# Sliding-window attention: the two tiles of a key head in turn, scores without padding, values of both tiles in one product

## The chip, the cores and the metric

One core of a Trainium2 chip runs the whole program, a two-layer decoder trunk. The metric is the time of one execution on the device, in microseconds (us). Engines are named as in the profile: PE (TensorE, matmuls), PEld (its weight loads), DVE (VectorE), ACT (ScalarE), POOL (GpSimd), SP (SyncE, which issues most of the transfers).

## What is computed

1024 tokens of width 1024 pass a short gated convolution, a SwiGLU layer, an attention and another SwiGLU layer, each behind an RMSNorm and with a residual. The change lies in the attention: 16 query heads of 64, four key heads, each query sees the 128 latest keys, with a distance bias and a learned sink per head.

```python
q = rmsnorm(q, q_gain)      # (b, s, 4 key heads, 4 queries per key head, 64)
k = rmsnorm(k, k_gain)
qb = q.reshape(bsz, nb, BLOCK, N_KV_HEADS, GROUP, HEAD_DIM)      # blocks of 128 queries
kw, vw = band(k), band(v)                                        # 256 keys per block
scores = jnp.einsum('bnqkgd,bnskd->bnkgqs', qb, kw) * scale
scores = scores - slopes * dist                                  # dist = i + 128 - j
scores = jnp.where((dist >= 0) & (dist < 128) & (key_pos >= 0), scores, -jnp.inf)
p = jax.nn.softmax(concat([scores, sink_col]), axis=-1)[..., :-1]
out = jnp.einsum('bnkgqs,bnskd->bnqkgd', p, vw)
return out.reshape(bsz, s, 1024) @ w_o
```

## The kernel before

Every float32 operand is split into a high and a low part, and a product is three matmuls of parts (high by high, high by low, low by high) of up to 512 columns. The big products (input, gate, down) use a scheme with sums of quarter matrices; they are not touched.

**Tiles and units.** The 16 query heads make eight tiles `i` of two heads. A tile belongs to one key head, and a key head has two tiles. A unit `(i, b)` is a tile and a block `b` of 128 queries. In a unit, `e` or `sub` are the two halves of 64 queries; each half sees 192 keys (fewer in the first block). The stationary operand of a half's scores holds two heads x 64 queries in its 128 columns, and high and low parts of a query share the 128 rows, so that two matmuls (L2234, L2235) make the scores of a half.

**Order of the units.** `units` runs tile by tile, in each through its eight blocks. `HEADS` puts the heads so that neighbouring tiles have different key heads: tile `i` uses half `i % 2` of the keys' operand `kz[i // 4]`.

**A unit's way.** `scores` writes bank P0. `maxima` (DVE, L2249) adds the bias, takes the minimum of negated scores and writes them to one of three buffers in SBUF (`s_bufs`); `exponents` (ACT, L2269) follows. Each buffer is 2 x 256 wide: a half's 192 columns stand in it at 0 or at 64, and the remaining 64 are zeros, written once by POOL. `turn` (PE, L2277) transposes the four blocks of 128 x 128 to a bank, P1 or P3 (two in block 0), `turn_hi` (ACT, L2284) and `turn_lo` (DVE, L2290) split the result into a tile `G0` or `G1`. `values` (PE, L2303, L2304) multiplies each 128-key block of V, high and low parts of its 64 columns side by side, by the 256 columns of both halves. `keep_o` (ACT L2321, DVE L2322) adds the two parts of the result to the output tile `O`.

**The order of instructions** is written out by hand. `step` issues for one `n` what the letters of `ORDER` say: S scores, M maxima and E exponents of units n, n and n-1, T, H and L (turn and its split) of unit n-2, V and O (values and keep) of unit n-3, D the divisions that are due, k and K what `plan` put on this step, and P a piece of the products that go on beside it. While the units run, PE's other work comes in such pieces: the query projections of the next tiles (`work_of_pairs`, L1997, in granules of 12 matmuls whose weights DVE or ACT (L1940) and POOL (L1941) split) and then the products of the output weights (`product_step`, L172, L176). The units begin `LAG` steps behind the pieces; with `full=False` a step has only a piece.

**Queries.** `keep_q` takes a finished query tile through squares (ACT, L2135), head sums (PE, L1678), mean, root (DVE L1685 to L1711, ACT L1697, L1702), a wide copy (POOL, L1803), a transposition to rows (PE, L1808), the scaling (DVE, L1813) and the split into high parts (ACT, L2165) and low parts (POOL, L2170), with steps counted from `later`. The even tile of a pair of query tiles is finished before the odd one; the odd one's last sum is L1986. The key operand's parts are made by `part` (L1873 to L1880; its low part on POOL, L1878).

Each engine takes its instructions in the order in which they were issued.

Of the kernel before, what the change touches and what calls it, by code (L numbers as in the profile page):

```python
# [15 lines left out]
P = 128  # L16
D = 1024
T = 1024
# [13 lines left out]
TILES = [0, 2, 1, 3, 4, 6, 5, 7]  # L32
HEADS = [2 * i + e for i in TILES for e in range(2)]
# [19 lines left out]
LAG = 4  # L53
# [6 lines left out]
ORDER = "SPTMEDkPHLVOPK"  # L60
# [28 lines left out]
def trunk_kernel(ctx: ExitStack, tc: tile.TileContext, xT, small, w_in, w_out, w_q, w_v, w_o, w_gu, w_dn, out):  # L89
# [748 lines left out]
    xres = [tc.dram_tile((P, T), F32, name=f"xres{m}") for m in range(NK)]  # L838
    first_sums = [tc.dram_tile((4, GROUP, P, 5 * P), F32, name=f"s1_{l}") for l in range(2)]
# [820 lines left out]
    def attention_layer():  # L1660
# [156 lines left out]
        def score_buffers():  # L1817
            g2 = slot("G2")
            s_bufs.append(slot("s0", (P, 2, 2 * P)))
            s_bufs.extend(g2[:, h * 512 : h * 512 + 512].rearrange("p (e c) -> p e c", e=2) for h in (0, 1))  # L1820
            for s in s_bufs:
                pool.memset(s[:, 0, KEYS:], 0.0)
                pool.memset(s[:, 1, 0:SUB], 0.0)

        def keys_and_values():
# [18 lines left out]
            at(t - 20.0, constants)  # L1844
            for q in (0, 1):
                load(("wv", q), w_v[:, 4 * q : 4 * q + 4, :], 4, t + (-14.0, -12.5)[q])
                at(t + (-9.3, -6.6)[q], split_v, q)
# [54 lines left out]
        PT = {}  # L1902
        PV = {}
# [51 lines left out]
        def raw_of_odd(u):  # L1955
            if u == KEYS_AS_PAIR:
                if 1 not in key_raw:
                    key_raw[1] = slot("G4")
# [166 lines left out]

        def keep_q(i, raw_of, side=None, later=0, steps=False):
# [3 lines left out]
            def squares(h):  # L2130
                if "raw" not in t:
                    t["raw"] = raw_of()
                    wide = slot(f"G{5 + i % 2}") if side is None else side
# [27 lines left out]
            def part_hi(h, e):  # L2161
                rows, _ = halves(e)
                if e == 0:
                    Q.setdefault(i, []).append(slot(f"G{(3, 5)[h] + i % 2}", (P, 8, 2, SUB), F32R))
# [61 lines left out]
        def scores(i, b):  # L2226
            hi, lo = kz[i // 4]
            g = i % 2
# [9 lines left out]
        def maxima(i, b):  # L2238
            u = S[i, b]
            s = s_bufs[(i * NB + b) % 3]  # L2240
# [3 lines left out]
            for sub in (0, 1):  # L2244
                _, n = sub_keys(b, sub)
                end = (3 + sub) * SUB
                live = s[:, sub, end - n : end]
# [23 lines left out]
        def turn(i, b):  # L2271
            s = S.pop((i, b))["s"]
            own, pos["free"] = ("P1", "P3") if b % 2 else ("P3", "P1")
            ps = bank(own).rearrange("p (k e c) -> p k e c", k=2, e=2)
            for kb in key_blocks(b):
                for e in range(2):
                    pe.transpose(ps[:, kb, e, :], s[:, e, kb * P : (kb + 1) * P], ident)  # L2277
            PT[i, b] = ps

        def turn_hi(i, b):  # L2280
            ps = PT[i, b]
            both = slot(f"G{b % 2}", (P, 2, 2, 2, P), F32R)
            f = key_blocks(b)[0]
            act.copy(both[:, 0, f:], ps[:, f:])  # L2284
            PT[i, b] = (ps, both)

        def turn_lo(i, b):
            ps, both = PT[i, b]
            f = key_blocks(b)[0]
            dve.tensor_tensor(both[:, 1, f:], ps[:, f:], plain(both[:, 0, f:]), ALU.subtract)  # L2290

        def values(i, b):
            both = PT.pop((i, b))[1]
            th, tl = both[:, 0], both[:, 1]
            kbs = key_blocks(b)
            g = 2 * (i // 4) + i % 2
            ps = pos["values"] if b % 2 and pos["values"] else bank("P2")
            ps = ps[:, 0 : 2 * P].rearrange("p (e c) -> p e c", e=2)
            for n, kb in enumerate(kbs):
                blk = b - 1 + kb  # L2300
                first, last = n == 0, n == len(kbs) - 1
                vb = v[blk // 4][:, blk % 4, g].rearrange("p l d -> p (l d)")
                pe.matmul(ps, vb, th[:, kb], start=first, stop=False)  # L2303
                pe.matmul(ps, vb, tl[:, kb], start=False, stop=last)  # L2304
            p = i // 2
# [367 lines left out]
```

## Time and profile before

| | |
|---|---|
| time, median of 3 runs | 1925.99 us (1924.19 to 1926.29) |
| span of the profiled execution | 1921.5 us |
| median less that span | 4.5 us |
| granted clock of PE | 1.000 |
| the attention's units in the span (first scores to last output copy) | 1027 to 1237 us |
| idle time of PE in the span, 1921.5 - 1910.4 | 11.1 us |

The profile was taken in one execution; its own time is not given apart from its span, so the 4.5 us stand for what lies around a span. Busy times count an instruction from start to modelled end, and PE's overlap: the pitch of a matmul is read from rows that follow one another, not from its mean. A row of the timeline has the start, the time from the first start to the last end, the engine, the line, operation, output <- inputs, the shape, the count, and in brackets the idle time ahead of it with what ended it. A row of a group has busy time and mean ns behind its count, and after the second bar the idle time ahead of the group and what ended most of it.

### The profile page before, as it was taken

How to read it: one execution, taken by the hardware profiler on the slowest of the kernel's cores; microseconds unless marked ns; L12 is line 12 of the kernel's file. 1: busy time of each engine (PE TensorE's matmuls, PEld its weight loads, DVE VectorE, ACT ScalarE, POOL GpSimd, SP SyncE). 2: the span in 40 equal slices, each digit the busy share in tenths (PEclk: the TensorE clock that was granted, in tenths of full speed). 3: DMA queues.
4: the chain of work that ended last, by engine and by line, in shares of the span. 5: the costliest groups of instructions: out<-in, count | busy, mean ns of one | idle time of the engine just before them, and what ended most of it. 6: DMA issues, size and time to landing. Idle time of an engine off the chain costs nothing.

```text
span 1921.5 us, 25423 instructions
## 1 busy us (share of the span) xinstructions
PE 1910.4 (99%) x9045; PEld 1595.6 (83%) x9045; DVE 1323.1 (69%) x2293; ACT 891.6 (46%) x1753; POOL 305.9 (16%) x391
## 2 busy tenths in 40 slices
PE   9999999999999999999999999999999999999999
PEld 7888888888888888888887888888888888888887
DVE  8998877975655666555767888788756665665543
ACT  5543464633333334444557787556333333344441
POOL 0011231011111100000015556310111111100000
PEclk9999999999999999999999999999999999999999
DMA  8896695387888647986374661232675575477562
GB/s 317 258 251 149 133 249 160 110 274 209 228 250 234 152 141 281 325 249 211 102 257 158 210 214 50 94 137 89 216 204 144 196 200 158 130 251 269 198 228 100
DMA packets 154910, 374.13 MB, mean 195 GB/s; under 512 B 15392, under 2 KB 26784, under 8 KB 154784
## 3 DMA queue, kind: packets, MB, share of 16 engines
q1 hardware_dynamic: 119392, 263.16, 40.1%
q0 software_dynamic: 35248, 109.33, 23.4%
q8 instruction: 71, 1.16, 0.2%
q14 instruction: 55, 0.45, 0.1%
q10 hardware_dynamic: 144, 0.03, 0.0%
HBM read 300.89 MB, written 149.42 MB: 234 GB/s over the span
## 4 chain that ended last, share of the span: by engine, by line
PE 96%; DVE 2%; ACT 1%; issue 1%; POOL 0%; DMA 0%; SPq 0%; POOLq 0%; ACTq 0%; DVEq 0%
PE acc L1004 16%; PE acc L1007 16%; PE acc L1005 16%; PE P L1004 10%; PE P L1005 10%; PE P L1007 10%; PE acc L172 3%; PE acc L1997 2%; PE P L1997 2%; PE acc L176 1%; PE P L2277 1%; PE P L1678 1%; PE P L1808 1%; PE acc L1137 1%; PE acc L1139 1%; PE acc L1138 1%
## 5 line engine op out<-in xcount | busy, mean ns | idle before, releaser
L1004 PE MATMUL acc<-XS,G 128*128 128x512 f32 x926 | 360.4, 389 | 0.0
L1005 PE MATMUL acc<-XS,G 128*128 128x512 f32 x926 | 360.2, 389 | 0.0
L1007 PE MATMUL acc<-XS,G 128*128 128x512 f32 x926 | 360.2, 389 | 0.0
L1004 PE MATMUL P<-A,G 128*128 128x512 f32 x550 | 214.1, 389 | 0.0
L1007 PE MATMUL P<-A,G 128*128 128x512 f32 x550 | 214.0, 389 | 0.0
L1005 PE MATMUL P<-A,G 128*128 128x512 f32 x550 | 214.0, 389 | 0.0
L1007 PEld LDWEIGHTS acc<-XS,G 128*128 128x128 f32 x926 | 173.8, 188 | 36.2
L1005 PEld LDWEIGHTS acc<-XS,G 128*128 128x128 f32 x926 | 173.8, 188 | 36.1
L1004 PEld LDWEIGHTS acc<-XS,G 128*128 128x128 f32 x926 | 173.8, 188 | 36.0
L1004 PE MATMUL acc<-A,G 128*128 128x512 f32 x442 | 172.1, 389 | 0.0
L1007 PE MATMUL acc<-A,G 128*128 128x512 f32 x442 | 172.0, 389 | 0.0
L1005 PE MATMUL acc<-A,G 128*128 128x512 f32 x442 | 171.9, 389 | 0.0
L938 DVE TENSOR_TENSOR G<-WL,G 128x512 fp32r<-128x512 f32 x168 | 115.2, 685 | 73.2 <-ACT G L937 73.2
L938 DVE TENSOR_TENSOR G<-WR,G 128x512 fp32r<-128x512 f32 (+1 forms) x216 | 144.4, 668 | 30.6 <-ACT G L937 30.6
L937 ACT CAST G<-WR 128x512 fp32r<-128x512 f32 (+1 forms) x216 | 130.5, 605 | 62.3 <-PE acc L1007 31.4
L937 ACT CAST G<-WH 128x512 fp32r<-128x512 f32 (+1 forms) x174 | 104.6, 601 | 88.5 <-PE acc L1007 38.2
L938 DVE TENSOR_TENSOR G<-WH,G 128x512 fp32r<-128x512 f32 (+1 forms) x174 | 115.6, 665 | 23.3 <-ACT G L937 23.2
L1339 ACT ACTIVATE G<-G 128x512 f32<-128x512 f32 x88 | 55.8, 634 | 158.5 <-DVE G L1436 152.7
L1007 PEld LDWEIGHTS P<-A,G 128*128 128x128 f32 x550 | 103.2, 188 | 21.5
L1004 PEld LDWEIGHTS P<-A,G 128*128 128x128 f32 x550 | 103.2, 188 | 21.4
L1005 PEld LDWEIGHTS P<-A,G 128*128 128x128 f32 x550 | 103.2, 188 | 21.4
L901 POOL DMA_DIRECT2D s<-s x68 | 60.0, 892 | 365.3 <-DMA s<-s 179.5
(414 smaller groups left out, 3794.2 us busy)
## 6 DMA issues: line engine op xcount, KB each, us to landing
G<-h SPq DMA_DIRECT2D x70, 512.0 KB, 4.5
s<-in_w_dn SPq DMA_DIRECT2D x32, 704.0 KB, 8.4
h<-X POOLq DMA_DIRECT2D x44, 512.0 KB, 4.8
s<-s POOLq DMA_DIRECT2D x32, 704.0 KB, 7.1
WR<-s SPq DMA_DIRECT2D x79, 256.0 KB, 3.9
WR<-in_w_gu SPq DMA_DIRECT2D x36, 512.0 KB, 5.1
WH<-in_w_gu SPq DMA_DIRECT2D x36, 512.0 KB, 4.2
XS<-q_ops SPq DMA_DIRECT2D x36, 512.0 KB, 5.1
```

What stands on the lines that cost most here:

```text
L172: pe.matmul(ps.half(h), wh, xs[:, j, c], start=first and j == 0, stop=False)
L176: pe.matmul(ps.half(h), wl, xs[:, 0, c], start=False, stop=last)
L901: nc.gpsimd.dma_start(dst[to], dst[of], accum_op=ALU.add)
L937: lambda: act.copy(out_hi, raw),
L938: lambda: lo_eng.tensor_tensor(out_lo, raw, plain(out_hi), ALU.subtract),
L1004: pe.matmul(ps, w[:, 0, c], x[:, 0, :], start=start and e == 0, stop=False, skip_group_check=True)
L1005: pe.matmul(ps, w[:, 0, c], x[:, 1, :], start=False, stop=False, skip_group_check=True)
L1007: pe.matmul(ps, w[:, 1, c], x[:, 0, :], start=False, stop=last, skip_group_check=True)
L1137: pe.matmul(ps, hi[:, kc], xs[:, 0, c], start=k == 0, stop=False, skip_group_check=True)
L1138: pe.matmul(ps, hi[:, kc], xs[:, 1, c], start=False, stop=False, skip_group_check=True)
L1339: state["silu"] = act.activation(x, x, AF.Silu)
L1997: pe.matmul(ps, g[:, w, c], x[:, b, :], start=begin and i == 0, stop=end and i == 2, skip_group_check=True)
```

## The change

**The units change order.** `HEADS` is the plain order, so tiles 2p and 2p+1 share a key head, and `units` runs pair by pair, in each block by block, and in each block through both tiles. `LAG` is 6.

**The scores stand without padding.** A buffer is 384 wide: 192 columns of the first half of the queries, then 192 of the second. Cut at 128, these are: the first half's keys in block b-1; its 64 keys in block b beside the second half's 64 in block b-1; the second half's keys in block b. `turn` makes three transpositions (two in block 0).

**The values of both tiles are one product.** The split of a pair's two units goes to a common tile, `parts`, of 3 blocks x 2 tiles x 128. For each half of the queries `values` takes one block of V in full and 64 rows of the other, and 256 columns that are both tiles. The first half's product stands in the step as `v`, the second's as `V` one step on; outputs follow as `o` and `O`.

**Room.** With two tiles of queries live at once more room is needed. Three tiles of x, X5 to X7, are copied to DRAM (`x_aside`) ahead of the attention and brought back in its last part, and their rooms hold keys, squares and parts in between. The preparation of the odd query tile moves: `later=-1` for tile 1 instead of 4, -0.5 for later odd tiles instead of 3 or 2, and 1 instead of 0 for even ones. Divisions are due at other steps, and more of the last steps hold units.

```diff
-TILES = [0, 2, 1, 3, 4, 6, 5, 7]
-HEADS = [2 * i + e for i in TILES for e in range(2)]
+HEADS = list(range(NH))
...
-LAG = 4
+LAG = 6
...
-ORDER = "SPTMEDkPHLVOPK"
+ORDER = "vSPVTMEDkoPHLOPK"
...
-            s_bufs.append(slot("s0", (P, 2, 2 * P)))
+            s_bufs.append(slot("s0", (P, 2 * KEYS)))
...
+            for m in x_aside:
+                at(t + 9.0 + 2.0 * (m - NK + 3), lambda m=m: nc.sync.dma_start(x_aside[m], X[m]))
...
-            s = S.pop((i, b))["s"]
-            own, pos["free"] = ("P1", "P3") if b % 2 else ("P3", "P1")
-            ps = bank(own).rearrange("p (k e c) -> p k e c", k=2, e=2)
-            for kb in key_blocks(b):
-                for e in range(2):
-                    pe.transpose(ps[:, kb, e, :], s[:, e, kb * P : (kb + 1) * P], ident)
-            PT[i, b] = ps
+            u = S.pop((i, b))
+            own, pos["free"] = ("P1", "P3") if i % 2 else ("P3", "P1")
+            ps = bank(own)
+            for blk in range(b == 0, 3):
+                c = slice(blk * P, (blk + 1) * P)
+                pe.transpose(ps[:, c], u["s"][:, c], ident)
+            PT[i, b] = ps.rearrange("p (k c) -> p k c", c=P)
...
+            p, e = i // 2, i % 2
+            if e == 0:
+                parts[p, b] = [slot(part_tag(p, b, l), (P, 3, 2, P), F32R) for l in (0, 1)]
+            f = int(b == 0)
+            act.copy(parts[p, b][0][:, f:, e, :], PT[i, b][:, f:3])
...
-            for n, kb in enumerate(kbs):
-                blk = b - 1 + kb
-                first, last = n == 0, n == len(kbs) - 1
-                vb = v[blk // 4][:, blk % 4, g].rearrange("p l d -> p (l d)")
-                pe.matmul(ps, vb, th[:, kb], start=first, stop=False)
-                pe.matmul(ps, vb, tl[:, kb], start=False, stop=last)
...
+        def values(p, b, sub):
+            if sub == 0:
+                ps = pos["values"] if b % 2 and pos["values"] else bank("P2")
+                PV[p, b] = ps.rearrange("p (s e c) -> p s e c", s=2, e=2)
+                terms = [(b - 1, 0, slice(0, P)), (b, 1, slice(0, SUB))]
+            else:
+                terms = [(b, 2, slice(0, P)), (b - 1, 1, slice(SUB, P))]
+                if pos["n"] > NU:
+                    PV[p, b, 1] = bank("P0").rearrange("p (s e c) -> p s e c", s=2, e=2)
+            terms = [t for t in terms if t[0] >= 0]
+            ps = PV.get((p, b, sub), PV[p, b])[:, sub]
+            todo = [(blk, k, rows, part) for blk, k, rows in terms for part in parts[p, b]]
+            for n, (blk, k, rows, part) in enumerate(todo):
+                vb = v[blk // 4][rows, blk % 4, p].rearrange("p l d -> p (l d)")
+                pe.matmul(ps, vb, part[rows, k], start=n == 0, stop=n == len(todo) - 1)
...
-        units = [(i, b) for i in range(NK) for b in range(NB)]
+        units = [(2 * p + e, b) for p in range(NK // 2) for b in range(NB) for e in range(2)]
...
+                "v": lambda: value(5, 0),
+                "V": lambda: value(6, 1),
+                "o": lambda: rest(6, 0),
+                "O": lambda: rest(5, 1),
...
-                                keep_q(2 * u, lambda u=u: raw_of_even(u))
+                                keep_q(2 * u, lambda u=u: raw_of_even(u), later=1)
...
-                                keep_q(2 * u + 1, lambda raw=raw: raw, side, later=3 if u + 1 < NK // 2 else 2)
+                                keep_q(2 * u + 1, lambda raw=raw: raw, side, later=-0.5)
...
-            keep_q(1, lambda: rooms["odd"], later=4)
+            keep_q(1, lambda: rooms["odd"], later=-1)
...
+                    if m == 2 and k == 0:
+                        last_x_back()
...
-                    step(work, full=(k != REST or m in (2, 5)) and pos["n"] < NU + 3)
+                    step(work, full=(k != REST or m in (1, 2, 4, 5, 6)) and pos["n"] < NU + 5)
```

The lines of the changed program are numbered anew: scores L2245 and L2246, maxima L2260, turns L2288, values L2323, query products L2004, low parts of weights L1948, of queries L2181 and of keys L1884.

How the instructions move is shown at three places. First PE in the units of the first tile, before (`acc_...` with `WL` are pieces, `P0` the scores, `G0` and `G1` the turned and split scores, `A4` the values):

```order
L2277 MATMUL P3_1222_8591<-cst_1_61,G2_1187_8365 128x128 x4
L1997 MATMUL acc_1194_8415<-XS5_1115_7592,WL_1140_7847 128x512
L1997 MATMUL acc_1194_8415<-XS7_1118_7619,WL_1140_7847 128x512
L2303 MATMUL acc_1195_8416<-G1_1216_8563,A4_1181_8306 128x256
L2304 MATMUL acc_1195_8416<-G1_1216_8563,A4_1181_8306 128x256
L2303 MATMUL acc_1195_8416<-G1_1216_8563,A4_1181_8306 128x256
L2304 MATMUL acc_1195_8416<-G1_1216_8563,A4_1181_8306 128x256
```

And PE in the units of the first pair after the change (`X6`, `G1` are the high and the low parts of both tiles in odd blocks):

```order
L2323 MATMUL acc_1195_8419<-X6_1224_8634,A4_1181_8312 128x256
L2323 MATMUL acc_1195_8419<-G1_1225_8635,A4_1181_8312 128x256
L2323 MATMUL acc_1195_8419<-X6_1224_8634,A4_1181_8312 128x256
L2323 MATMUL acc_1195_8419<-G1_1225_8635,A4_1181_8312 128x256
L2288 MATMUL P3_1239_8745<-cst_1_61,s0_1188_8372 128x128 x3
L2004 MATMUL acc_1194_8418<-XS2_1106_7537,WL_1139_7849 128x512
```

A unit's turns are three instead of four; the four products of a step stand as before, but the last two of each four read 64 rows of their operands (the program places them in a half of the array of 64 x 128), and belong to two units. In the whole program PE has 184 turns instead of 240, and 240 value products in both, 120 of which have 64 rows now, in 60 runs of two.

Second, PE from the last products of tile 0's half to the scores of unit 1, after the change (`G3` and `G4` are query tiles 0 and 1, `X5` tile 1's squares and wide roots; the first row here stands in both programs, and there the next is a row of products):

```order
L2004 MATMUL acc_1192_8416<-XS6_1117_7606,WL_1139_7849 128x512 x3
L1678 MATMUL P3_1202_8450<-cst_1_61,X5_1200_8437 128x2 x8
...
L2004 MATMUL acc_1194_8418<-XS6_1117_7606,WL_1140_7850 128x512 x2
L1808 MATMUL P3_1206_8493<-cst_1_61,X5_1200_8437 128x128 x4
...
L1808 MATMUL P3_1208_8513<-cst_1_61,X5_1200_8437 128x128 x4
...
L2245 MATMUL P0_1209_8525<-A0_1177_8278,G3_1190_8398 128x64
...
L2245 MATMUL P0_1214_8549<-A0_1177_8278,G4_1207_8504 128x64
```

The statistics and the two turns of tile 1 stand ahead of the first scores now; before, they stood behind the scores of units 3, 5 and 6, and tile 1's queries were read first at unit 8.

Third, POOL at the same place, before (`WL` granules, `G3`, `G5` halves of tile 0, `A2`, `A3` keys):

```order
L1941 TENSOR_TENSOR WL_1140_7847<-WR_1135_7842,WL_1140_7847 128x512
L2170 TENSOR_TENSOR G3_1190_8395<-G7_1176_8270,G3_1190_8395 64x8x64
L2170 TENSOR_TENSOR G5_1200_8440<-G7_1176_8270,G5_1200_8440 64x8x64
L1941 TENSOR_TENSOR WL_1139_7846<-WR_1135_7842,WL_1139_7846 128x512
L2170 TENSOR_TENSOR G5_1200_8440<-G7_1176_8270,G5_1200_8440 64x8x64
L1878 TENSOR_TENSOR A2_1178_8273<-G1_1161_8073,A0_1177_8272 64x1024
```

And after the change:

```order
L1948 TENSOR_TENSOR WL_1140_7850<-WR_1135_7845,WL_1140_7850 128x512
L2181 TENSOR_TENSOR G3_1190_8398<-G7_1176_8276,G3_1190_8398 64x8x64
L2181 TENSOR_TENSOR G5_1201_8446<-G7_1176_8276,G5_1201_8446 64x8x64
L1803 COPY X5_1200_8437<-hr_y_1204_8461 128x512
L1948 TENSOR_TENSOR WL_1139_7849<-WR_1135_7845,WL_1139_7849 128x512
L2181 TENSOR_TENSOR G5_1201_8446<-G7_1176_8276,G5_1201_8446 64x8x64
L1803 COPY X5_1200_8437<-hr_y_1204_8461 128x512
L1948 TENSOR_TENSOR WL_1140_7850<-WR_1135_7845,WL_1140_7850 128x512
L1884 TENSOR_TENSOR A2_1178_8279<-G1_1161_8079,A0_1177_8278 64x1024
L2181 TENSOR_TENSOR G4_1207_8504<-WH_1138_7848,G4_1207_8504 64x8x64 x2
```

The wide copies and the low parts of tile 1 (`G4`) have come in between; before, they stood among and behind the keys' three low parts. The low part of the keys `A2` written here is that of the second key head, which unit 16 reads first now and unit 8 before.

More of the change, by code (lines that the diff above doesn't have):

```diff
@@ L1902, in attention_layer @@
         PT = {}
+        parts = {}
         PV = {}
@@ L2239, in maxima @@
             u = S[i, b]
-            s = s_bufs[(i * NB + b) % 3]
+            s = s_bufs[units.index((i, b)) % 3]
             if i % 2 == 0 and b % 4 == 0:
@@ L2287, in turn_lo @@
-        def turn_lo(i, b):
[L2288 to L2298, printed above, removed]
-            for n, kb in enumerate(kbs):
-                blk = b - 1 + kb
-                first, last = n == 0, n == len(kbs) - 1
-                vb = v[blk // 4][:, blk % 4, g].rearrange("p l d -> p (l d)")
-                pe.matmul(ps, vb, th[:, kb], start=first, stop=False)
-                pe.matmul(ps, vb, tl[:, kb], start=False, stop=last)
-            p = i // 2
-            if b == 0 and i % 2 == 0:
+            u = S.pop((i, b))
@@ L2312, in values @@
                     O[p, 0], O[p, 1] = both[:, 0], both[:, 1]
-            PV[i, b] = ps
         def keep_o(i, b):
-            ps = PV.pop((i, b))
             rows = slice((i % 2) * HD, (i % 2 + 1) * HD)
             o = O[i // 2, b // 4][rows, :, (b % 4) * P : (b % 4 + 1) * P].rearrange("p e (s q) -> p s e q", q=SUB)
-            ps = ps.rearrange("p s (e q) -> p s e q", q=SUB)
-            act.copy(o, ps[0:HD])
-            dve.tensor_tensor(o, ps[HD:P], o, ALU.add)
+            own = PV.get((i // 2, b, 1))
+            for s in (slice(0, 2),) if own is None else (slice(0, 1), slice(1, 2)):
+                ps = own if own is not None and s.start else PV[i // 2, b]
+                ps = ps[:, s, i % 2].rearrange("p s (e q) -> p s e q", q=SUB)
+                act.copy(o[:, s], ps[0:HD])
+                dve.tensor_tensor(o[:, s], ps[HD:P], o[:, s], ALU.add)
         def divide_steps(p, h, k):
@@ L2393, in step, with value, rest @@
             at = lambda d, f: f(*units[n - d]) if full and 0 <= n - d < NU else None
+            def value(d, sub):
+                if full and 0 <= n - d < NU and (n - d) % 2 == 0:
+                    i, b = units[n - d]
+                    values(i // 2, b, sub)
+            def rest(d, e):
+                if (n - d) % 2 == e:
+                    at(d, keep_o)
             pos["piece"] = 0
@@ L2547, in attention_layer @@
                 w = w_next
-            assert pos["n"] == NU + 3 and not todo
+            assert pos["n"] == NU + 5 and not todo
             while agenda:
```

47 lines of the change are left out of this document (28 added, 19 removed).

## The prediction

> **What bounds the kernel now.** I read the page first, then the table of stretches over the attention, then who waits for whom there, then single rows of the timeline. The page's busy times and its chain:
>
> ```profile
> PE 1910.4 (99%) x9045; PEld 1595.6 (83%) x9045; DVE 1323.1 (69%) x2293; ACT 891.6 (46%) x1753; POOL 305.9 (16%) x391
> ...
> PE 96%; DVE 2%; ACT 1%; issue 1%; POOL 0%; DMA 0%; SPq 0%; POOLq 0%; ACTq 0%; DVEq 0%
> ```
>
> TensorE (PE) is the bound: 99% busy, 96% of the chain. So an instruction taken from PE is worth its pitch, and what the other engines save is worth nothing unless PE waits for them. Where it waits is read from the stretches of the attention (columns: us, then PE, PEld, DVE, ACT, POOL busy with counts, clock, DMA share, GB/s):
>
> ```profile
> 1018.00:1036.00 18.00, 15.97 (x79) 11.93 (x77) 12.71 (x31) 15.46 (x36) 10.52 (x7) 1.00 0.69 247
> 1036.00:1061.00 25.00, 23.14 (x160) 20.35 (x161) 19.78 (x58) 19.57 (x55) 14.96 (x12) 1.00 0.35 111
> 1061.00:1100.00 39.00, 38.60 (x269) 34.54 (x269) 34.43 (x107) 31.00 (x98) 22.15 (x25) 1.00 0.64 211
> 1100.00:1150.00 50.00, 49.59 (x347) 44.42 (x346) 43.80 (x131) 40.29 (x127) 27.59 (x30) 1.00 0.63 208
> 1150.00:1200.00 50.00, 49.03 (x330) 43.12 (x328) 40.55 (x118) 38.50 (x118) 31.84 (x36) 1.00 0.18 59
> 1200.00:1242.00 42.00, 42.00 (x253) 36.46 (x252) 32.24 (x82) 27.54 (x83) 13.55 (x19) 1.00 0.16 53
> ```
>
> PE idles 2.03 + 1.86 = 3.9 us in the first two stretches, where the attention starts, and 0.40 + 0.41 + 0.97 = 1.8 us in all the rest. The granted clock is 1.00 throughout, so no term here comes from it. The waits behind the idle time (total, times, longest):
>
> ```profile
> PE P L2234 <- DVE mx L2249: 2.4, 4, 1.0
> PE acc L1997 <- POOL WL L1941: 1.7, 2, 1.4
> ```
>
> PE waits for VectorE to free the scores' bank, and for POOL's low parts of the weights. The start is thus the one place where the order of small work on POOL and DVE decides the time.
>
> **Term 1: the turns that go.** The counts and a quiet unit late in the attention:
>
> ```profile
> L2277 PE MATMUL P<-cst,G 128*128 128x128 f32 x158 | 24.1, 272 | 0.0
> ...
> L2277 PE MATMUL P<-cst,s 128*128 128x128 f32 x82 | 12.5, 272 | 0.0
> ```
> ```profile
> 1219.33 0.25 PE L2234 MATMUL P<-A,G 128*128 128x192 f32 x1
> ...
> 1219.76 0.64 PE L172 MATMUL acc<-XS,WH 128*128 128x512 f32 x2
> 1220.24 0.60 PE L2277 MATMUL P<-cst,G 128*128 128x128 f32 x4
> 1220.59 0.71 PE L172 MATMUL acc<-XS,WH 128*128 128x512 f32 x2
> 1221.14 0.28 PE L2303 MATMUL P<-G,A 128*128 128x256 f32 x1
> ...
> 1221.62 0.63 PE L176 MATMUL acc<-XS,WL 128*128 128x512 f32 x2
> ```
>
> 158 + 82 = 240 turns: 56 units of four and 8 (the first block of each tile) of two. After the change the 56 have three: 56 turns go. A turn is not worth its 272 ns, which overlap; four take 0.60 us from first start to last end, so the pitch is (0.60 - 0.272) / 3 = 0.109 us. The matmul behind does not win it back: the two of L172 after the turns show 0.71 where the two before show 0.64. **56 x 0.109 = 6.1 us less**, all on PE and so all on the path.
>
> **Term 2: the values.** They stay 240 matmuls of 256 columns; four lie between 1221.14 and 1221.62, a pitch of 0.12 us. New is that 120 of them read 64 rows. No instruction of the trace has fewer than 128, so the price is bounded. Below: a matmul of half the rows might cost half, 120 x 0.06 = 7 us less; but each still streams 256 columns, and nothing in the rows shows a matmul cheaper for having less to sum, so I give that end little weight. Above: PE might not overlap a matmul with one of another height. Then each border shows the overlapped part, 0.28 - 0.12 = 0.16 us. The 120 lie in 60 runs of two, so 120 borders, 19.2 us more. I take 0, the nearest row being these same 256 columns at 0.12, and keep the upper end as a rival.
>
> The Trainium skill, TensorEngine Tiling (Array Packing), section Key Properties, speaks against the change here: changing the tiling mode drains TensorE, and this program does place those 120 in a mode of 64 x 128. By it the 19.2 us would be due, without it nothing; no run so far shows which. The skill's TensorE: Matmul & The Clock Gate, section LDWEIGHTS, says that a weight load goes by columns and not rows, by which the half-height matmuls would keep their 0.12.
>
> **Term 3: lighter VectorE and ScalarE.** The split of the turned scores (512 columns now, 384 then; 256 in the first blocks):
>
> ```profile
> L2290 DVE TENSOR_TENSOR G<-P,G 128x512 fp32r<-128x512 f32 x56 | 38.5, 687 | 13.8 <-ACT G L2284 13.6
> ...
> L2290 DVE TENSOR_TENSOR G<-P,G 128x256 fp32r<-128x256 f32 x8 | 3.4, 423 | 1.7 <-ACT G L2284 1.6
> ```
> ```profile
> L2284 ACT CAST G<-P 128x512 fp32r<-128x512 f32 x56 | 32.1, 573 | 7.6 <-PE P L2277 7.4
> ...
> L2284 ACT CAST G<-P 128x256 fp32r<-128x256 f32 x8 | 2.8, 353 | 0.0
> ```
>
> Half way between: 0.13 us less on DVE and 0.11 on ACT for each of 56 units. PE's step shortens by 0.109 too, so their share of a step stays about as it is. It can only touch the 1.8 us of waits after the start; I take **0.3 us less**, between 0 and 1.8.
>
> **Term 4: the start.** Here the change costs. Tile 1's queries are needed as unit 1 instead of unit 8, so all their preparation moves ahead of the first scores, into six steps that hold only three pieces of a product each. The rows it is made of:
>
> ```profile
> 1023.18 0.60 PE L1808 MATMUL P<-cst,G 128*128 128x128 f32 x4
> 1023.53 3.90 PE L1997 MATMUL acc<-XS,WL 128*128 128x512 f32 x16
> ```
> ```profile
> 1017.58 0.17 DVE L1685 SCALAR_TENSOR_TENSOR hr_m<-P,eps_r 128x16 f32<-128x16 f32 x1 [0.78 <-PE P L1678]
> ...
> 1020.42 0.18 DVE L1711 SCALAR_TENSOR_TENSOR hr_y<-hr_t,hr_y 128x16 f32<-128x16 f32 x1
> ...
> 1025.34 0.69 DVE L1986 TENSOR_TENSOR WH<-WH,P 128x512 f32<-128x512 f32 x1
> 1025.95 1.66 DVE L1796 SCALAR_TENSOR_TENSOR A<-acc,r,A 128x256 fp32r<-128x256 f32 x4
> ```
> ```profile
> L1941 POOL TENSOR_TENSOR WL<-WR,WL 128x512 fp32r<-128x512 f32 x21 | 27.3, 1302 | 36.4 <-DVE WL L1940 8.7 <-PE P L2277 8.1 <-ACT WL L1940 7.3
> L2170 POOL TENSOR_TENSOR G<-G,G 64x512 fp32r<-64x512 f32 x15 | 19.4, 1290 | 2.9 <-ACT G L2165 2.0
> ...
> L1803 POOL COPY G<-hr_y 128x512 f32<-128x512 f32 x12 | 7.2, 611 | 12.0 <-PE P L1808 6.1 <-DVE hr_y L1711 5.8
> L1878 POOL TENSOR_TENSOR A<-G,A 64x1024 fp32r<-64x1024 f32 x3 | 7.2, 2390 | 0.2
> ```
> ```profile
> L2135 ACT ACTIVATE G<-WH 128x512 f32<-128x512 f32 x6 | 3.7, 623 | 0.0
> ...
> L1678 PE MATMUL P<-cst,G 128*128 128x2 f32 x96 | 11.2, 247 | 0.3 <-DVE G L2290 0.3
> ```
>
> PE's products have a pitch of (3.90 - 0.39) / 15 = 0.23 us; four turns take 0.44, eight statistics 8 x 0.117 = 0.9, a unit's scores 0.43 (1219.33 to 1219.76). Both kernels are alike up to 1023.53. From there, by the order of the changed program:
>
> - (a) After 7 products (1025.2) PE stands at tile 1's statistics. Its squares need the sum of L1986, done at 1026.03, and take 0.62: 1026.7. A wait of 1.5.
> - (b) The statistics end at 1027.7. From a mean (L1685) to its root (L1711) the rows above take 3.0 us with DVE busy in between; 2.3 without. Then POOL copies it wide in 0.61, until 1030.7. PE has had 11 products (2.5) and stands since 1030.2. A wait of 0.5.
> - (c) The second half needs, on POOL, a granule's low part 1.30, a query low part 1.29 and a copy 0.61: 1034.0. PE has a turn and five products, 0.44 + 1.2: 1032.4. A wait of 1.6.
> - (d) Unit 1's scores need tile 1's two low parts. POOL has ahead of them a granule, 1.30, and a low part of the keys that only tile 2 uses, 2.39; with 2 x 1.29 they end at 1040.3. PE has a turn, nine products and unit 0's scores, 0.44 + 2.1 + 0.43: 1037.0. A wait of 3.3.
> - (e) POOL then carries 1.30 + 2.39 + 2.58 + 2.39 before the next granule's 1.30 (1050.2), and PE reaches that near 1050. A wait of 0 to 0.6, taken as 0.3.
>
> Sum 7.2 us. A wait shows as idle less the overlapped tail of 0.16, five times 0.8: 6.4 us of idle where the start has 3.9 now (0.1 of it ahead of 1023.53). The waits of now, for POOL's granules and for DVE, come from the same pile and are replaced, not added. **2.6 us more**, between 0 (the pile drains in the waits themselves, and later units find it gone) and 5.
>
> **Edits at nothing.** Three tiles of x go to DRAM and back, 1.5 MB each way: the stretch from 1150 has a DMA share of 0.18, and the attention reads them only in its last sums. If the return were late, the next output weights, issued behind it on SP's queue, would come late: up to 1 us. Leaving fewer products behind the last unit (3.5 us of them instead of 5) is covered by those that follow in the channel mixer. Twelve narrower output copies, two for one, lie on ACT and DVE at shares of 27.5 and 32.2 in 42.
>
> **Sum.** -6.1 - 0.3 + 2.6 = -3.8, and 0.1 for the split output copies: -3.7 us. The profiled span is 1921.5; the timed median lies 4.5 above it, taken as what surrounds the span. 1921.5 - 3.7 + 4.5 = **1922.3 us**. A measurement of this kernel can tell about 0.2%, 3.9 us, from no change: this forecast lies just within.
>
> **The rivals.**
> - *The mode border stalls PE* (slower). At 120 borders of 0.16 us each: 1922.3 + 19.2 = 1941.5. It decides from 3.7 / 120 = 0.031 us a border. For it: PE's overlap is worth more than half of each of these matmuls, and nothing in the trace shows it kept between unlike heights. Against it: nothing shows it lost. With 0.03 to 0.06 it gives 1926 to 1930. Chance 0.22, of which the full price 0.14.
> - *The start costs nothing extra*: the present waits there vanish with the pile they come from and the new ones are no larger. 1921.5 - 6.1 - 0.3 + 4.5 = 1919.6. For it: DVE, ACT and POOL have 18% to 40% to spare after 1061. Against it: POOL's row in (d) is a plain sum. Chance 0.17.
> - *POOL comes late at each new pair too*: at units 16, 32 and 48 two tiles of queries must be ready within one unit, where now one is. By POOL's sum there (five pieces, 6.5 us, in two steps and one to spare of 2.75) it just holds; 1 us late at each gives 1925.3. Chance 0.11.
> - *Something outside the attention*, the extra transfers above all, costs 3 to 10 us: 0.05.
> - That the turns or the values aren't what the change says is excluded by the order: 184 turns and 240 products.
>
> **Chances.** The forecast holds 0.45, from 1920.0 to 1924.5; 0.19 of that is faster by over 0.2%. Faster 0.19 + 0.17 = 0.36. Within 0.2%: 0.26 + 0.11 + 0.03 of the small borders = 0.40. Slower 0.24. The range leaves out the full border price and thin tails: 1918.5 to 1932.0.
>
> **What would show it.** In the trace after: 184 turns with a pitch of 0.109; the pitch of the 64-row products and of the matmul behind them, 0.12 if free and 0.28 if not; PE idle of 6 to 7 us before unit 2, longest ahead of unit 1's scores with POOL's low part as releaser; at most 1.8 us of idle later. The prediction is wrong if PE's time between a full and a half product exceeds 0.15 us, or if unit 1 finds its queries ready.

## The result and the profile after

| | before | after |
|---|---|---|
| time, median | 1926.04 us (4 runs, 1924.19 to 1926.29) | 1969.96 us (4 runs, 1969.74 to 1972.62) |
| ratio to before, 95% interval | | 1.0232, 1.0217 to 1.0246 |
| span of the profiled execution | 1921.5 us | 1968.0 us |
| granted clock of PE, mean | 1.000 | 0.994 |

The change makes the kernel 2.3% slower, where 1922.3 us was predicted. The 46.5 us of span lie between 1018 and 1290 us; outside, the two traces agree to 0.3 us. PE is still the bound: the page's busy times, after:

```profile
PE 1939.8 (99%) x8989; PEld 1603.4 (81%) x8989; DVE 1321.8 (67%) x2299; ACT 891.2 (45%) x1759; POOL 306.2 (16%) x388
```

Busy time of PE rose by 29 us for 56 fewer instructions, so part of the loss hides in busy time, and the rest, 17 us, is idle time. The stretches of the attention, after (columns as before the change: us, then PE, PEld, DVE, ACT, POOL busy with counts, clock, DMA share, GB/s):

```profile
1018.00:1036.00 18.00, 14.85 (x76) 10.79 (x75) 9.69 (x24) 12.94 (x25) 8.83 (x8) 1.00 0.56 174
1036.00:1061.00 25.00, 21.41 (x110) 17.60 (x108) 18.26 (x49) 16.78 (x46) 17.36 (x11) 0.86 0.38 127
1061.00:1100.00 39.00, 37.46 (x229) 30.35 (x227) 28.15 (x89) 26.71 (x87) 21.02 (x23) 1.00 0.70 230
1100.00:1150.00 50.00, 49.84 (x289) 41.17 (x290) 37.09 (x116) 33.94 (x108) 20.50 (x22) 0.93 0.56 179
1150.00:1200.00 50.00, 46.50 (x284) 37.84 (x283) 35.62 (x106) 34.00 (x107) 28.55 (x31) 1.00 0.29 91
1200.00:1250.00 50.00, 42.48 (x216) 33.41 (x216) 29.46 (x88) 25.89 (x85) 14.43 (x21) 0.90 0.11 38
```

Three different losses can be read off. From 1100 to 1150 PE is busy 49.84 of 50 us, but does 289 instructions where it did 347: each takes longer. From 1150 on PE stands idle for 3.5 to 7.5 us in 50, where it stood for at most 1. And the clock, 1.00 before throughout, is 0.86, 0.93 and 0.90 in three stretches. The waits of PE between 1018 and 1290 (total, times, longest):

```profile
PE P L2323 <- DVE A L2340: 7.7, 6, 2.1
PE P L2323 <- DVE XS L2340: 4.8, 6, 1.4
...
```

These two rows, 12.5 us, are the values (L2323) waiting for the additions that end the output copies (L2340). The prediction has no such wait. The waits at the start come with their rows in the part on the prediction.

**Where the time went.** To add these up, every PE instruction of the stretch was given the distance of its end from the end of the one before it, less the distance that its shape has in a quiet place (0.227 us for 512 columns, 0.118 for 256, about 0.11 for fewer). What is left over sums to 11.6 us before and 63.9 after; 63.9 - 11.6 - 6.1 for the turns that went is 46.2, the 46.5 of the span. By what stands at each place, after:

| what | us |
|---|---|
| borders (steps between matmuls of 64 and of 128 rows), 113 at full clock | 20.2 |
| values waiting for their bank, 12 times | 15.5 |
| half clock (a granted clock of 0.50; with 1.8 of borders in it) | 10.3 |
| the rest: start, other waits, small distances (11.6 before) | 17.9 |

**The borders.** The timeline of PE, one run of four value products and the turns behind it, after:

```profile
1102.75 0.28 PE L2323 MATMUL acc<-X,A 128*128 128x256 f32 x1
1102.87 0.28 PE L2323 MATMUL acc<-G,A 128*128 128x256 f32 x1
1103.08 0.38 PE L2323 MATMUL acc<-X,A 64*128 64x256 f32 x1
1103.30 0.28 PE L2323 MATMUL acc<-G,A 64*128 64x256 f32 x1
1103.51 0.55 PE L2288 MATMUL P<-cst,s 128*128 128x128 f32 x3
```

The two full products are 0.12 us apart. Into the half-high ones the end moves from 1103.15 to 1103.46, 0.31 instead of 0.12: 0.19 lost. Inside the run it moves by 0.12 again. Out of it, too, the first start is 0.21 behind the last one instead of 0.12. So it isn't the half-high matmul that is dear but the step from one height to the other, about 0.18 us on average. By the ends, the 56 steps into half height lose a median of 0.19 us; the 57 out of it lose 0.15 ahead of a turn, 0.18 ahead of scores and 0.20 ahead of a product.

**The wait for the bank.** The timeline of PE, DVE and ACT late in the attention, after, from the last product of one `V` to the next `v` (not all rows):

```profile
1226.38 0.28 PE L2323 MATMUL P<-G,A 64*128 64x256 f32 x1
...
1226.69 0.37 ACT L2339 COPY A<-P 64x256 f32<-64x256 f32 x1 [2.06 <-PE P L2323]
...
1227.61 0.69 DVE L2368 TENSOR_TENSOR A<-A,P 128x512 f32<-128x512 f32 x1 [1.18 <-PE P L1808]
...
1227.88 0.62 PE L175 MATMUL acc<-XS,WL 128*128 128x512 f32 x2
1228.21 0.25 DVE L2357 RECIPROCAL den<-den 128x16 f32<-128x16 f32 x1
1228.49 0.42 DVE L2340 TENSOR_TENSOR A<-P,A 64x256 f32<-64x256 f32 x1
...
1228.95 0.56 DVE L2307 TENSOR_TENSOR G<-P,G 128x384 fp32r<-128x384 f32 x1
1228.95 0.36 ACT L2339 COPY A<-P 64x256 f32<-64x256 f32 x1 [1.30 <-DVE A L2340]
...
1229.54 0.43 DVE L2340 TENSOR_TENSOR A<-P,A 64x256 f32<-64x256 f32 x1
...
1230.11 0.47 PE L2323 MATMUL P<-G,A 64*128 64x256 f32 x2 [1.62 <-DVE A L2340]
```

In the part with the output weights the program has one bank for the values (`pos["values"]` is None, so `bank("P2")` every time). Both tiles' outputs must be copied out of it, one behind the other: the second copy (ACT at 1228.95) waits for the first tile's addition on DVE, then comes its own addition, until 1229.97, and only then may the next `v` write. And `v` is the first letter of `ORDER`: it stands at the head of the step right behind the one that has both `o` and `O`, with only one piece of products (`P`) between `O` and it. The two copies and two additions take 1.6 us, but the round from 1226.66 to 1230.11 takes 3.45: in between VectorE does what stands ahead of the additions in its own order, a division's scaling (L2368), a reciprocal (L2357) and the split of the turned scores (L2307). The twelve rounds with a wait take 2.0 to 4.7 us, and L2307 stands in each.

**The half clock.** PE, ahead of and in a stretch of half clock, after:

```profile
1127.87 1.92 PE L1678 MATMUL P<-cst,X 128*128 128x2 f32 x16 [0.16 <-DVE G L1813]
1129.65 0.41 PE L2245 MATMUL P<-A,G 128*128 128x192 f32 x1
1129.86 0.42 PE L2246 MATMUL P<-A,G 128*128 128x192 f32 x1
```

The scores follow one another at 0.21 instead of 0.11. The clock record shows 0.5 from 1041.0 for 6.8 us, from 1129.8 for 6.8, from 1201.4 for 6.8 and from 1221.9 for 3.4; before the change there is none in the attention of the profiled execution.

### The profile page after: what moved, and what is told of

Same layout as the page of the kernel before. It is cut to its first block, busy times and chain, and to the rows that moved or that the text cites. A ratio compares the mean times of both kernels' runs of the same rounds, so it can differ in the third digit from the quotient of the medians.

```text
span 1968.0 us, 25314 instructions
## 1 busy us (share of the span) xinstructions
PE 1939.8 (99%) x8989; PEld 1603.4 (81%) x8989; DVE 1321.8 (67%) x2299; ACT 891.2 (45%) x1759; POOL 306.2 (16%) x388
## 4 chain that ended last, share of the span: by engine, by line
PE 93%; DVE 3%; ACT 2%; POOL 1%; issue 1%; DMA 0%; ACTq 0%; POOLq 0%; DVEq 0%
PE acc L1004 16%; PE acc L1005 16%; PE acc L1007 16%; PE P L1004 9%; PE P L1005 9%; PE P L1007 9%; PE acc L171 2%; PE P L2004 2%; PE acc L2004 2%; PE P L2323 1%; PE P L2288 1%; PE P L1678 1%; PE acc L175 1%; PE P L2245 1%; PE acc L1139 1%
## 5 line engine op out<-in xcount | busy, mean ns | idle before, releaser
L937 ACT CAST G<-WR 128x512 fp32r<-128x512 f32 (+1 forms) x216 | 130.7, 606 | 66.7 <-PE acc L1007 24.4
```

The lines of the kernel that those rows point to most:

```text
L937: lambda: act.copy(out_hi, raw),
```

## Experiments

Times are medians beside runs of the kernel before on the same chip: 1924.06 us for the first four experiments (two executions each), 1925.94 for the last three (three each). Ratios are to the kernel before. "Left over" is the sum described above.

| run | us | ratio, 95% interval | borders | bank wait | half clock |
|---|---|---|---|---|---|
| after | 1969.96 | 1.0232, 1.0217 to 1.0246 | 20.2 | 15.5 | 10.3 |
| e1_full_height | 1957.98 | 1.0173, 1.0143 to 1.0202 | 0 | 15.3 | 13.7 |
| e2_more_borders | 1991.48 | 1.0347, 1.0317 to 1.0377 | 42.6 | 14.1 | 11.9 |
| e3_outputs_early | 1969.24 | 1.0231, 1.0202 to 1.0261 | 21.1 | 10.8 | 7.5 |
| e4_keys_behind | 1970.41 | 1.0237, 1.0208 to 1.0267 | 20.2 | 15.5 | 10.6 |
| e5_full_and_late | 1945.55 | 1.0100, 1.0078 to 1.0121 | 0 | 1.3 | 6.8 |
| e6_all_three | 1945.15 | 1.0099, 1.0079 to 1.0119 | 0 | 1.3 | 8.1 |

**1. No border: all products in full height.**

```diff
-                vb = v[blk // 4][rows, blk % 4, p].rearrange("p l d -> p (l d)")
-                pe.matmul(ps, vb, part[rows, k], start=n == 0, stop=n == len(todo) - 1)
+                vb = v[blk // 4][:, blk % 4, p].rearrange("p l d -> p (l d)")
+                pe.matmul(ps, vb, part[:, k], start=n == 0, stop=n == len(todo) - 1)
```

> Each value product reads all 128 rows of its operands, so that no matmul has another height than its neighbours (the sums then hold 64 foreign keys each, so the output is not the reference's). Theory (PE cannot load the next weights across a change of the array's tiling, 120 borders of 0.18 us): the 22 us of the borders go, and with fuller use of PE some of the half-clock stretches: 1938 to 1950 us, the pitch of all value products 0.12 us. Rival (the 46 us are the late start and the shared values bank alone, the border price is an artefact of the modelled ends): 1966 to 1970 us.

Measured: 1957.98 us. The same place in this run, PE:

```profile
1102.43 0.28 PE L2323 MATMUL acc<-X,A 128*128 128x256 f32 x1
1102.55 0.28 PE L2323 MATMUL acc<-G,A 128*128 128x256 f32 x1
1102.66 0.28 PE L2323 MATMUL acc<-X,A 128*128 128x256 f32 x1
1102.78 0.28 PE L2323 MATMUL acc<-G,A 128*128 128x256 f32 x1
1102.90 0.27 PE L2288 MATMUL P<-cst,s 128*128 128x128 f32 x1
```

The borders are gone without a trace: 0.12 throughout. But only 12 us came back for 22 of borders (20.2 and 1.8), and the time lies between the ranges of the theory and of the rival. PE now reaches the other engines' work sooner. Its waits in this run:

```profile
PE P L2323 <- DVE A L2340: 6.8, 6, 2.0
PE P L2323 <- DVE XS L2340: 5.2, 7, 1.4
...
PE P L2245 <- DVE mx L2260: 3.3, 6, 0.8
PE P L2288 <- DVE WH L1813: 2.9, 2, 1.5
```

The waits for the scores' bank (L2260) and of the turns for the scaling of the next queries (L1813) grew, from 0.9 us of idle time each to 3.3 and 2.9, and the half clock from 10.3 to 13.7.

**2. More borders: the same products, with the heights alternating.**

```diff
-            todo = [(blk, k, rows, part) for blk, k, rows in terms for part in parts[p, b]]
+            todo = [(blk, k, rows, part) for part in parts[p, b] for blk, k, rows in terms]
```

> The same 240 products, but full and half heights alternate within each half's sum: 56 groups of four have three borders more inside instead of one (232 borders instead of 120, same operands, same result). Theory (price per border, 0.18 us): 112 x 0.18 = 20 us more, 1985 to 1995 us. Rival (price per half-high matmul, 120 x 0.37 / 2): no change, 1968 to 1972 us.

Measured: 1991.48 us, 21.5 more than the change. There are 232 borders instead of 120, 112 more: 0.19 us each. The trace says the same, 42.6 us at 228 of them. The products are the same in number, shape and result, and in run 1, with the operands in the order of the change and equal heights, nothing is lost. This settles that the price is one of the border.

**3. Outputs earlier: the second tile's copies ahead of the piece.**

```diff
-ORDER = "vSPVTMEDkoPHLOPK"
+ORDER = "vSPVTMEDkoOPHLPK"
```

> In each step the second tile's output (copy and addition) is issued right behind the first's, ahead of the split of the turned scores. Theory (in the last part all values share one bank, and the next values wait for the second output's addition; 12 waits, 15.5 us): each wait is shorter by 0.5 to 1.1 us, the time 5 to 13 us less, 1957 to 1965 us, and PE's wait for L2340 falls from 12.5 us idle to under 6. Rival (VectorE is the bound there, so that whatever moves ahead delays something else): 1968 to 1973 us with the wait moved to the scores or the turns.

Measured: 1969.24 us, not told apart from the change. The waits for the bank fell only from 15.5 to 10.8 (from 12.5 us of idle time to 8.4, not under 6), and others grew with the copies ahead of `L`: PE's waits for L1813 rose from 1.2 us of idle time to 2.8 and those for L2260 from 0.9 to 1.6. The rival was nearer: moving the copies up in VectorE's crowded order didn't give the bank the slack that it needs.

**4. Unit 1's queries ahead of the second key head's keys on POOL.**

```diff
-                for i, dd in enumerate((0, 0, 1.5 if g == 0 else 1, 4.5 if g == 0 else 3)):
+                for i, dd in enumerate((0, 0, 3 if g == 0 else 1, 4.5 if g == 0 else 3)):
```

> POOL's low part of the second key head, which unit 16 reads first, is issued behind tile 1's two low parts instead of ahead of them. Theory (the wait ahead of unit 1 is POOL's sum): that wait falls from 3.6 us idle to 0.5 to 1.5, and the half-clock stretch that follows it goes too: 4 to 6 us less, 1964 to 1966 us. Rival (POOL's pile is only moved on): the same wait appears at a granule within 10 us, 1969 to 1971 us.

Measured: 1970.41 us, no gain. The rows of PE's timeline at the start that have a wait:

```profile
1035.67 0.66 PE L1808 MATMUL P<-cst,X 128*128 128x128 f32 x4 [0.59 <-POOL X L1803]
1039.62 0.30 PE L2245 MATMUL P<-A,G 128*128 128x64 f32 x1 [0.76 <-POOL G L2181]
1043.29 0.36 PE L2245 MATMUL P<-A,G 128*128 128x192 f32 x1 [1.80 <-DVE mx L2260]
```

Unit 1's wait fell from 3.59 to 0.76, which shows that POOL's low part of the keys (2.39 us) stood in its way, as step (d) has it. But 1.80 of it came back at once at unit 2, where VectorE hasn't freed the scores' bank. The half clock near the start didn't go either: it is 0.5 from 1030.2 and from 1043.8 for 3.4 us each, as long together as the 6.8 us from 1041.0 before this edit. The rival is right that the pile moves on, though to VectorE and not to a granule.

**5. No border, and `v` late in the step.** As in 1, and

```diff
-ORDER = "vSPVTMEDkoPHLOPK"
+ORDER = "SPVTMEDkovPHLOPK"
```

> As in the run with full-height products, every value product reads 128 rows, so the sums hold 64 foreign keys each and the output is not the reference's. In addition v stands behind the products of the step instead of at its head, so that the bank of the values in the last part has most of a step to come free. Theory (the borders and the wait for the values' one bank are two separate costs, and the wait also thins PE's stream and so brings half-clock stretches): the waits of the values' line on the copies fall from 15 us to under 4, the half-clock cost of 13.7 us to under 6, and the time is 1938 to 1946. Rival (the wait only moves on to the turns and the scores, since DVE and ACT are too late by themselves in this order): the sum of PE's waits for DVE and ACT stays within 4 us of what it was with full height alone, and the time is 1953 to 1960.

Measured: 1945.55 us, at the upper end of the theory's range, 12.4 below run 1 (14 by the two ratios). The half clock, 6.8, stayed above the 6 of the theory. PE's waits:

```profile
PE P L2288 <- DVE WH L1813: 3.9, 2, 1.9
PE P L2245 <- DVE mx L2260: 3.6, 8, 0.7
PE P L2245 <- POOL G L2181: 3.5, 1, 3.5
...
PE P L2323 <- DVE A L2340: 0.3, 1, 0.3
```

The values hardly wait any more, 1.3 us left over for 15.3, and the waits for L1813 and L2260 didn't take that over. So `v` at the head of the step was a cost by itself. The same order with half-high products wasn't tried.

**6. All three: 5, and the keys behind as in 4.**

> As e5_full_and_late (output not the reference's for the same reason), and the first low part of the second key head's keys is moved behind tile 1's low parts on POOL. Theory: unit 1's wait falls from 3.6 us to about 0.8, and with PE's stream not thinned elsewhere nothing eats it: 2 to 3 us below e5_full_and_late. Rival (the pile on POOL only moves on): within 1.5 us of it.

Measured: 1945.15 us, the same as 5. The wait for POOL's low parts falls from 3.5 to 0.8 and that for L2260 rises from 3.6 to 5.4 us of idle time; the half clock is 8.1 instead of 6.8. The rival again. With the borders and the bank wait gone and the queries early, the order of the change is still 1% slower than before. 38.9 us are left over in this run, 11.6 before: waits for L2260 8.1, half clock 8.1, L1813 6.0, the other waits of the start 4.6, and 12 in smaller ones. No run points to a version that beats the kernel before.

**7. The clock, in the kernel before: PE kept busy, but with few columns.** Matmuls of 2 columns, of no use, behind the turns of steps 20, 36 and 52, and transpositions of 128 columns at step 28:

```diff
             for c in ORDER:
                 calls[c]()
+                if c == "T" and full and n in (20, 28, 36, 52):
+                    spare = bank(pos["free"])
+                    for _ in range({20: 34, 28: 34, 36: 18, 52: 10}[n]):
+                        if n == 28:
+                            pe.transpose(spare[:, 0:P], ident, ident)
+                        else:
+                            pe.matmul(spare[:, 0:2], ident, half, start=True, stop=True)
```

> The kernel before with useless PE work at four steps: at step 20, 34 matmuls of 2 columns (3.8 us at 0.112); at step 28, 34 transpositions of 128 columns (3.7 us at 0.109); at step 36, 18 matmuls of 2 columns (2.0 us); at step 52, 10 of them (1.1 us). PE never waits for them and counts as busy throughout. Theory (the clock falls to half after a stretch of about 3.4 us in which PE streams few columns, busy or not): a half-clock stretch follows step 20 and none follows step 28, though both keep PE busy for the same time; step 52 gives none; step 36 is open. Time 1924 plus 10.6 us of work plus 3 to 4 us for one such stretch, 1936 to 1941. Rival (the clock falls where PE is idle, not where it is thin): clock 1.00 throughout, 1934 to 1936.

Measured: 1951.12 us, ratio 1.0133 (1.0113 to 1.0153). The time lies above both expected ranges. Each of the matmuls of 2 columns is two instructions in the trace, which the expectation missed: 124 of them, 13.9 us at 0.112, and 3.7 for the 34 transpositions, 17.6 instead of 10.6. Its timeline at steps 20, 28 and 36:

```profile
1092.78 11.03 PE L2422 MATMUL P<-cst 128*128 128x2 f32 x68
...
1128.55 3.87 PE L2420 MATMUL P<-cst 128*128 128x128 f32 x34
...
1157.15 4.08 PE L2422 MATMUL P<-cst 128*128 128x2 f32 x36
```

And its stretches around them and behind step 52:

```profile
1092.00:1096.60 4.60, 4.60 (x42) 4.46 (x41) 1.91 (x7) 1.84 (x6) 1.87 (x2) 1.00 0.36 119
1096.60:1106.80 10.20, 10.05 (x46) 9.80 (x46) 1.29 (x2) 0.01 (x1) 0.00 (x0) 0.50 0.00 0
...
1128.00:1136.00 8.00, 7.85 (x66) 7.29 (x65) 4.37 (x13) 2.95 (x12) 0.86 (x3) 1.00 0.57 207
...
1161.40:1164.80 3.40, 3.40 (x14) 3.11 (x15) 1.54 (x3) 0.62 (x2) 0.00 (x0) 0.51 0.03 7
...
1219.50:1222.90 3.40, 3.40 (x15) 2.91 (x13) 1.31 (x5) 1.56 (x6) 0.72 (x1) 0.50 0.13 33
```

PE never stands for more than 0.15 us ahead of these. Behind the matmuls of 2 columns at steps 20, 36 and 52 the clock is 0.50; behind the transpositions, which follow one another at the same 0.11 us, it stays 1.00. That step 52 (20 instructions, 2.2 us) would do it wasn't expected. The rival, that the clock falls only where PE is idle, is out. The time above the useless work, 1951.1 - 1925.9 - 17.6 = 7.6 us, is of the size of the half clock's cost in the profiled execution, about 11. Two of its stretches, from 1038.6 and from 1062.5, lie ahead of step 20, where nothing was added; each follows a tile's statistics of 2 columns. So the order before can have half clock too; the mean clocks of that kernel's runs reach from 0.998 to 1.000.

## Why the prediction was wrong, step by step

Between the forecast, 1922.3 us, and the measurement lie 47.7 us. Three costs that the forecast put at nothing, the borders (20.2), the values' bank (15.5) and the half clock (10.3), make 46.0 of them in the profiled execution. Taking away the first two (runs 1 and 5) gave back 24.4 us and not their sum, since other waits grew in their place.

**The bound: right.** PE is 99% busy, and each loss was one of PE's time.

**Term 1, the turns: right.** 184 turns stand in the trace, and three of them,

```profile
1106.80 0.49 PE L2288 MATMUL P<-cst,G 128*128 128x128 f32 x3
```

have a pitch of (0.49 - 0.272) / 2 = 0.109. The 6.1 us went, and are needed for the sum to come out.

**Term 2, the values: the step that failed.** "I take 0" was wrong; the rival that had the border price was nearer, but with 1941.5 us it would have come out 28 short. Run 2's 112 added borders give 0.19 us each, and run 1 has none left when the heights are equal. The step had bounded the cost from the overlapped part, 0.28 - 0.12 = 0.16 us, 19.2 in all, and given it a chance of 0.22 as a rival; the trace has a median of 0.19 (0.12 to 0.20), and 22 in all. It was off for choosing the end "nearest" to a row that shows only equal heights: that row holds no evidence on unlike ones. The rule of the Trainium skill, TensorEngine Tiling (Array Packing), Key Properties, that a change of tiling mode drains TensorE, agrees with the trace, which puts the price at 0.19 us going in and 0.15 to 0.20 coming out. What the Trainium skill, TensorE: Matmul & The Clock Gate, says under LDWEIGHTS, that a load's time goes by columns and not rows, agrees too: a load takes 0.18 us with 64 rows and 0.19 with 128 (rows at the end), and inside a run of half height the pitch stays 0.12. It says nothing of a border.

**"At most 1.8 us of idle later": failed, and no rival had it.** The costing of the output copies, 0.1 us because ACT and DVE have time to spare in 42 us, looked at shares of busy time. Elsewhere it misread them besides: the rival on the start gives VectorE 18% or more to spare after 1061, and the prediction's own table has it busy 34.43 of 39 us and then 43.80 of 50, which leaves 12%. What decides is the round of one bank: two copies and two additions in a row, 0.37 + 0.42 + 0.36 + 0.43 = 1.6 us by the rows, and whatever VectorE does between them, before the next product may write. Before, V and O stood side by side, so that a step of other PE work lay between the copies and the next V. The diff shows `pos["values"]` and the `v` at the head of `ORDER`; following the bank would have found it. Run 5 shows its size, 12.4 us of time together with the half clock that it brings.

**"No term here comes from the clock": failed.** Waits of 1 to 4 us and statistics thinned PE's stream enough to halve its clock, 10.3 us in the profiled execution.

**Term 4, the start: right in mechanism, and in size for the idle time.** PE's timeline at the start, after:

```profile
1027.01 1.95 PE L1678 MATMUL P<-cst,X 128*128 128x2 f32 x16 [1.34 <-ACT X L2146]
...
1033.28 0.73 PE L2004 MATMUL acc<-G,WL 128*128 128x512 f32 x2 [0.35 <-POOL WL L1948]
1035.38 0.66 PE L1808 MATMUL P<-cst,X 128*128 128x128 f32 x4 [1.37 <-POOL X L1803]
...
1042.16 0.42 PE L2245 MATMUL P<-A,G 128*128 128x64 f32 x1 [3.59 <-POOL G L2181]
```

Steps (a) to (d) had waits of 1.5, 0.5, 1.6 and 3.3, with the tails of 0.16: the rows have 1.34, 0.35, 1.37 and 3.59 idle, 6.65 in all, where the forecast was 6.4 with (e). The half clock from 1041.0 on, just ahead of the last of these rows, comes on top. One thing came out by luck: the statistics are 16 instructions and take 1.95 us, not 0.9, so (b)'s wait for the first wide copy vanished and a granule's took its place.

**Term 3 and the edits at nothing.** The 0.3 us can't be seen beside the new waits. Three tiles of x aside and back cost nothing that shows: none of PE's waits above ends with a transfer.

**Each new pair.** The rival "POOL comes late at each new pair" named the wrong engine and was small in this kernel: PE waits there for VectorE's scaling (L1813), 1.2 us. Without borders it is 4.6 (run 1). What would be the least cost of this order, with everything that waits moved to its best place, stays open.

## What to carry to other kernels

Before halving the height of some of the products, count the steps between heights, not the products: here two neighbours of unlike height cost 0.15 to 0.20 us of TensorE at each step, where a product of 512 columns takes 0.23. Where two results share a buffer that had been one result's, follow that buffer around once, from its last write through every reader to its next write, with the durations of the rows and with what else the readers do in between; their share of busy time is no answer. And a wait of 1 us or more on the bound engine may cost more than itself, where it thins the stream enough for the clock to fall.

## What was not expected of the hardware

**The clock goes by how much streams through TensorE in fixed windows of 3.41 us, not by whether it is busy.** In each of the eight traces (after and seven experiments), all stretches of half clock in the attention start whole multiples of 3.413 us apart. Cut at that grid, the windows between 1016 and 1300 us, by the columns of the matmuls that end in them, and by the clock of the next window:

| columns in the window | next at half clock | next at full clock |
|---|---|---|
| under 2400 | 27 | 0 |
| 2400 to 3000 | 22 | 21 |
| 3000 to 3400 | 3 | 38 |
| over 3400 | 1 | 546 |

At the pitch of 0.227 us per 512 columns a full window holds 7700; less than 2400, about a third of that, brought the half clock each time. Run 7 shows it with PE busy throughout: its matmuls of 2 columns leave windows of 32 to 60 columns at steps 20 and 36 and one of 2600 at step 52, while its transpositions lie in two windows of 5120 and 4608. Where matmuls are counted by their starts instead, half clock follows 26 of 28, 23 of 37, 4 of 33 and 0 of 560 windows: the fall with the columns stays, the exact bound doesn't. Where the grid falls differs from one execution to the next, so the same wait may halve the clock in one and not in another: the single runs of run 5 reach from 1941.65 to 1948.19 us, with mean clocks from 0.995 to 0.992. The Trainium skill, TensorE: Matmul & The Clock Gate, Part 1, has a free-running window of 3413 ns, and the traces agree; by its table the clock falls after an idle window, and here it fell after windows in which PE was busy all the time.

**Weight loads don't run ahead over a border.** PE's weight loads (PEld) for the products shown above, after:

```profile
1102.75 0.19 PEld L2323 LDWEIGHTS acc<-G,A 128*128 128x128 f32 x1
1103.08 0.18 PEld L2323 LDWEIGHTS acc<-X,A 64*128 64x128 f32 x1
1103.18 0.19 PEld L2323 LDWEIGHTS acc<-G,A 64*128 64x128 f32 x1
1103.50 0.31 PEld L2288 LDWEIGHTS P<-cst,s 128*128 128x128 f32 x3
```

Between equal heights the load starts 0.12 us ahead of its matmul (1102.75 for 1102.87, 1103.18 for 1103.30), beside the matmul before. At a border it starts with its own matmul (1103.08, and 1103.50 for 1103.51): what was hidden lies open. At all 113 borders at full clock the load starts at most 0.003 us ahead of its matmul, and none of them cost less than 0.115 us. The price goes with the load's own duration: 0.15 ahead of a turn, whose load takes 0.14, 0.18 ahead of scores, with 0.19, and 0.19 or 0.20 ahead of a product, with 0.18 or 0.19. Why the load starts late, the traces don't show.
